# Neighbourhood attention: one key order for both layouts, scores as 64-row products, the next pair's scores before this pair's mix

## The chip, the cores and the metric

The kernel runs on one core of one Trainium2 chip. The metric is device time in microseconds. Three runs of the kernel before gave a median of 2800.92 us (2799.02 to 2803.72). The core has five engines with instruction queues of their own: PE multiplies matrices (weights are loaded by separate instructions, PEld in the profile), DVE and ACT work elementwise from SBUF and PSUM, POOL works elementwise from SBUF, and SP issues transfers. [...]

## The reference

The program is a two-layer encoder over 16 meta tokens and 512 grid tokens, 2048 wide. The first layer (a state-space branch and a convolution branch) is not touched here. The second is a neighbourhood attention with 32 heads of 64: each token of an 8 x 64 grid sees all 8 rows of 16 columns around it, and the 16 meta tokens. Cut to what matters:

```
def neighbourhood_attention(q, k, v, rpb):
    ...
    def row_block(r):
        rs = jnp.clip(r - kh // 2, 0, rows - kh)
        k_rows = lax.dynamic_slice_in_dim(kg, rs, kh, axis=1)
        ...
        s = jnp.einsum("bqhd,bjkhd->bhqjk", q_row, k_rows).astype(jnp.float32) * scale
        ...
        s = s + jnp.transpose(bias, (0, 2, 1, 3))[None]
        s = jnp.where(col_mask[None, None, :, None, :], s, -jnp.inf)
        ...
        s_m = jnp.einsum("bqhd,bkhd->bhqk", q_row, km).astype(jnp.float32) * scale
        p = jax.nn.softmax(jnp.concatenate([s, s_m], axis=-1), axis=-1).astype(v.dtype)
        o = (jnp.einsum("bhqj,bjhd->bqhd", p[..., :kh * GRID_W], ...)
             + jnp.einsum("bhqm,bmhd->bqhd", p[..., kh * GRID_W:], vm))
```

The layer then computes `o * silu(z)`, where z is the fourth part of the input projection, the output projection, the residual, and a final norm.

## The kernel before

Everything is kept transposed: channels on the 128 partitions, tokens along the free dimension, grid tokens ordered column by column (8 rows of a column lie together). Products that need fp32 precision are made of three products in a reduced format: each operand is split into a high part (a rounded copy, made by ACT) and a low part (the rest, made by DVE), and high x high, high x low and low x high are summed in PSUM. This holds for the projections (`fetch`, line 189 on: `wh` by ACT at L196, `wl` by DVE at L199) and for the scores.

**Stage.** Queries, keys and values lie in DRAM (`vqk_d`) when the attention stage begins. It goes over 16 pairs of heads; one pair fills the 128 partitions, head 0 on the lower 64, head 1 on the upper 64. The 512 queries are cut into four windows of 128 queries (16 grid columns); a window needs 24 or 32 grid columns of keys and the 16 meta keys, 208 or 272 keys in all (NK is 272).

**A pair, before.** `Pair` loads keys, queries and values into single buffers (`tk`, `tq`, `vT`) and the bias strips of both heads (`bt`). `khigh` and `qhigh` make the high parts on ACT, head by head (L888, L905). `klow` (L890) makes the low part of the keys and then, on DVE, the copies that the products need: the keys of the two inner windows laid out with the meta keys ahead (`wins`, L853 and L855), and the high part copied to the other 64 partitions (L896). `qlow` (L907) writes the low part of the queries to the other 64 partitions. With that, one product of 128 rows computes high x high and low x high of a head together (L946), and one of 64 rows adds high x low (L947):

```
nc.tensor.matmul(pq[:, :NK], self.qs[a][:, w * P:(w + 1) * P], self.kk[a][:, cb:cb + NK], start=True, stop=False)
nc.tensor.matmul(pq[:, :NK], self.qs[a][hs, w * P:(w + 1) * P], self.kl[hs, cb:cb + NK], start=False, stop=True)
```

`bias` builds the bias and mask of a window on POOL (L931). A DVE instruction adds it to the scores and takes the extreme of each row (L949), ACT takes the exponential and the sum (L950), `norm` scales the rows (L958), `turn` transposes them on PE into PSUM (L969 to L977) and copies them to SBUF (DVE L978 and L981, ACT L979 and L980), `values` transposes the values (L919, L921), and `mix` multiplies both (L994). The result leaves PSUM on ACT (L996).

**Order.** PE, DVE, ACT and POOL follow the order written out in the loop at L1065; SP's order is chosen by the planner. Between the steps of a pair, `next(g)` puts chunks of twelve products of the gate's projection (L1008), so that PE has work of its own while the other engines prepare; each pair has four chunks. After every second pair, `silu` (L1025) applies SiLU to two gate panels on ACT, multiplies the outputs of two pairs on POOL (L1029) and stores them. In the last pair, `reload` and `refill` bring the gated outputs back for the output projection, whose first panel's chunks come from the same generator. The loop's order per pair is: scores of head 0, chunk, scores of head 1, norm, chunk, transposes of head 0, chunk, transposes of head 1, values and key preparation of the next pair, chunk, query preparation, mix.

PSUM has five rotating buffers under the tag `sm` for scores, transposed probabilities and transposed values, and one for the mix.

## Time and profile before

| | |
|---|---|
| median of 3 runs | 2800.92 us (2799.02 to 2803.72) |
| span of the profiled execution | 2800.9 us |
| PE busy | 2706.6 us, 97% |
| DVE busy | 2241.9 us, 80% |
| ACT busy | 1419.8 us, 51% |
| POOL busy | 518.7 us, 19% |
| first and last chunk of the gate's projection (L1008) | 2187.9 and 2613.6 us |
| transfers | 354.23 MB, mean 126 GB/s |

The profiled execution's own time is its span. A busy PE counts from the start of a product to its modelled end, and products overlap, so the busy share does not show how densely products follow each other; the distance between their starts does. PEclk in the views is the clock that PE was granted, 1.00 for full speed. In a timeline row stand the start, the duration, the engine, the line, and what the instruction writes and reads with its shape; "x4" means that rows of one kind were merged, and a bracket gives the idle time before it and what ended it. The chain of waits follows the end of the program back: each piece is what the rest waited for.

### The profile page before, as it was taken

To read this page: it belongs to the slowest core of one execution; us is meant where nothing else is said; L and a number is where in the kernel's file an instruction comes from. 1 tells how busy PE (TensorE), PEld (TensorE's weight loads), DVE (VectorE), ACT (ScalarE), POOL (GpSimd) and SP (SyncE) were. 2 spreads that over 40 slices of the span, in tenths; PEclk is the share of its full clock that TensorE was granted. 3 is DMA by queue.
4 is the path that set the end of the run, shared out by engine and by line. 5 is a ranking of instruction groups with operands and counts; after the bars stand their busy time and mean duration, and the time that the engine had idled before them with its cause. 6 is when DMAs were issued, how large, how long until landed. Compare 5 with 4: busy or idle time off the path is not lost. (4 is left out here: it accounts for less than half of the span.)

```text
span 2800.9 us, 52378 instructions
## 1 busy us (share of the span) xinstructions
PE 2706.6 (97%) x21100; PEld 2548.9 (91%) x21100; DVE 2241.9 (80%) x3182; ACT 1419.8 (51%) x2601; POOL 518.7 (19%) x495
## 2 busy tenths in 40 slices
PE   8999999999999999999999899999999999999897
PEld 8999999999999999999999899999999776766797
DVE  7786786968769699977888898888888876776786
ACT  5356576565765664256435355333333554555443
POOL 2000000000000011002334323212212323222322
PEclk9999999999999999999999999999999998998998
DMA  4222222222222224337547466333333533333644
GB/s 163 89 82 84 88 80 89 86 89 86 78 95 80 95 83 147 107 131 252 161 147 252 157 205 211 131 135 119 133 129 125 143 94 95 99 94 109 204 158 152
DMA packets 133218, 354.23 MB, mean 126 GB/s; under 512 B 15488, under 2 KB 27904, under 8 KB 132976
## 3 DMA queue, kind: packets, MB, share of 16 engines
q1 hardware_dynamic: 126144, 328.65, 36.6%
q0 software_dynamic: 6544, 22.17, 2.2%
q8 instruction: 165, 2.70, 0.4%
q14 instruction: 77, 0.63, 0.1%
q10 hardware_dynamic: 288, 0.07, 0.0%
HBM read 300.40 MB, written 50.43 MB: 125 GB/s over the span
## 5 line engine op out<-in xcount | busy, mean ns | idle before, releaser
L196 ACT ACTIVATE wh<-raw 128x1024 fp32r<-128x1024 f32 (+1 forms) x458 | 484.0, 1058 | 731.3 <-PE pb L216 281.1
L235 PE MATMUL ps<-rh,wh 128*128 128x264 f32 (+2 forms) x3536 | 739.7, 288 | 13.7 <-ACT rh L252 8.5
L235 PE MATMUL ps<-rh,wl 128*128 128x264 f32 (+2 forms) x3536 | 739.8, 288 | 0.5 <-DVE wl L199 0.5
L235 PE MATMUL ps<-rl,wh 128*128 128x264 f32 (+2 forms) x3536 | 735.8, 288 | 1.2 <-DVE rl L253 1.1
L199 DVE TENSOR_TENSOR wl<-raw,wh 128x1024 fp32r<-128x1024 f32 (+1 forms) x458 | 582.0, 1271 | 96.0 <-ACT wh L196 89.1
L235 PEld LDWEIGHTS ps<-rh,wh 128*128 128x128 f32 (+1 forms) x3536 | 555.0, 189 | 20.2 <-ACT rh L252 8.5
L235 PEld LDWEIGHTS ps<-rh,wl 128*128 128x128 f32 (+1 forms) x3536 | 554.4, 189 | 4.2 <-DVE wl L199 1.2
L235 PEld LDWEIGHTS ps<-rl,wh 128*128 128x128 f32 (+1 forms) x3536 | 552.2, 189 | 5.7 <-DVE rl L253 2.0
L216 PE MATMUL pb<-rh,wl 128*128 128x264 f32 (+1 forms) x1280 | 368.2, 288 | 12.0 <-DVE wl L199 11.5
L216 PE MATMUL pb<-rh,wh 128*128 128x264 f32 (+1 forms) x1280 | 367.0, 287 | 4.1 <-ACT wh L196 3.8
L216 PE MATMUL pb<-rl,wh 128*128 128x264 f32 (+1 forms) x1280 | 366.3, 286 | 0.0
L529 DVE SCALAR_TENSOR_TENSOR a<-up,prm,a 128x528 f32<-128x528 f32 x464 | 345.2, 775 | 2.3 <-ACT a L524 0.9
L216 PEld LDWEIGHTS pb<-rh,wl 128*128 128x128 f32 x1280 | 243.3, 190 | 16.3 <-DVE wl L199 16.1
L216 PEld LDWEIGHTS pb<-rh,wh 128*128 128x128 f32 x1280 | 244.4, 191 | 5.7 <-ACT wh L196 5.5
L216 PEld LDWEIGHTS pb<-rl,wh 128*128 128x128 f32 x1280 | 244.1, 191 | 0.0
L216 PE MATMUL pb<-ta,wh 128*128 128x264 f32 (+1 forms) x1280 | 235.9, 284 | 2.5 <-ACT wh L196 2.4
L216 PEld LDWEIGHTS pb<-ta,wh 128*128 128x128 f32 x1280 | 198.4, 189 | 3.8 <-ACT wh L196 3.8
L216 PE MATMUL pb<-ta,wl 128*128 128x264 f32 (+1 forms) x640 | 180.8, 285 | 0.5 <-DVE wl L199 0.2
L196 ACT ACTIVATE wh<-S 128x1024 fp32r<-128x1024 f32 x80 | 84.5, 1057 | 120.0 <-PE pb L216 87.9
L216 PE MATMUL pb<-tb,wh 128*128 128x264 f32 (+1 forms) x640 | 125.6, 293 | 10.3 <-ACT tb L1142 5.8
L931 POOL TENSOR_TENSOR bm<-cst,bt 128x256 f32<-128x256 f32 (+1 forms) x128 | 94.0, 763 | 201.0 <-DVE mx L949 195.4
L1008 PE MATMUL ps<-rh,wh 128*128 128x512 f32 x272 | 121.2, 445 | 1.1 <-ACT rh L249 1.1
(324 smaller groups left out, 4337.0 us busy)
## 6 DMA issues: line engine op xcount, KB each, us to landing
raw<-win SPq DMA_DIRECT2D x192, 512.0 KB, 3.7
raw<-oin SPq DMA_DIRECT2D x128, 512.0 KB, 3.7
raw<-wout SPq DMA_DIRECT2D x64, 512.0 KB, 4.1
raw<-oout SPq DMA_DIRECT2D x32, 512.0 KB, 3.8
srt<-h_d SPq DMA_DIRECT2D x38, 264.0 KB, 4.4
srt<-yz_d SPq DMA_DIRECT2D x32, 264.0 KB, 5.3
srt<-yb_d SPq DMA_DIRECT2D x32, 264.0 KB, 4.0
vqk_d<-cx SPq DMA_DIRECT2D x26, 264.0 KB, 2.0
```

What stands on the lines that cost most here:

```text
L196: nc.scalar.activation(wh, raw, AF.Copy)
L199: nc.vector.tensor_tensor(wl, raw, wh.bitcast(F32), op=ALU.subtract)
L216: nc.tensor.matmul(o, w[:, k, :], u[:, lo:lo + n], start=(k == 0 and j == 0), stop=(k == KH - 1 and j == 2))
L235: nc.tensor.matmul(ps[:M, n, :N], w[:, k, :], u[:, lo + n * N:lo + (n + 1) * N], start=(kk == 0 and j == 0), stop=(kk == KT - 1 and j == 2))
L529: nc.vector.scalar_tensor_tensor(a, u[:, j:j + L], wv(j), a, op0=ALU.mult, op1=ALU.add)
L931: nc.gpsimd.tensor_tensor(bm[:, n0:n0 + n * GR].rearrange("p (c r) -> p c r", r=GR), am[:, w, c0:c0 + n].unsqueeze(2).to_broadcast([P, n, ...
L1008: nc.tensor.matmul(ps, w[:, k, :], u[:, lo:lo + S], start=(kk == 0 and j == 0), stop=(kk == KT - 1 and j == 2))
```

## The change

The keys and values get one order in SBUF, with the meta tokens in it twice: columns 0 to 63 of the grid, the 16 meta tokens, grid columns up to 464, the meta tokens again, and the last 64. Every window is then one contiguous stretch (`WIN`), and three transfers each for `tk` and `vT` write that order, so that the copies on DVE go. The high and low parts are made for both heads at once, each head staying on its own 64 partitions (`high`, `low`). Scores are three products of 64 rows for each window and head, 24 a pair instead of 16, and the heads, and so the partition halves, alternate. They are 208 columns wide for the outer windows and 272 for the inner ones. `tk`, `tq`, `vT` have two buffers, `bt` four, and the bias tiles four for each window; an outer window's bias is now written by two POOL instructions, on both sides of the meta columns.

The loop's order changes too: bias of the next pair, both norms of this pair, transposes of head 0, high parts of the next pair, chunk, low parts, transposes of head 1, values, chunk, scores of the next pair's outer windows, chunk, scores of its inner windows, this pair's mix, SiLU, chunk. The first pair's scores stand ahead of the loop. In the last pair, twelve outputs are reloaded at its start instead of eight and later four, and the refills move with the chunks.

```diff
+WIN = ((0, 208, ((0, 0, 8), (80, 8, 16)), 64), (64, NK, ((16, 0, WC),), 0), (208, NK, ((0, 0, WC),), 256), (336, 208, ((0, 8, 16), (144, 24, 8)), 128))
...
-TQB = 1
...
-        bms = {}
-        for w, n, lo in ((0, 2, 0), (1, 3, 0), (3, 2, 192)):
-            wd_ = NM + (192 if w != 1 else 256)
-            bms[w] = [ak.tile([P, wd_], F32, name=f"bm{w}{i}") for i in range(n)]
+        bms, bmi = [], [0] * NWIN
+        for w, (_, n, _, m) in enumerate(WIN):
+            bms.append([ak.tile([P, n], F32, name=f"bm{w}{i}") for i in range(4)])
             for t in bms[w]:
-                nc.gpsimd.memset(t[:, lo:lo + NM], 0.0)
-        bms[2] = bms[1]
-        bmi = {id(bms[w]): 0 for w in (0, 1, 3)}
+                nc.gpsimd.memset(t[:, m:m + NM], 0.0)
...
-        def wins(dst, src, rows):
-            d = dst[:, 2 * NK:].rearrange("p (w n) -> p w n", w=2)
-            nc.vector.tensor_copy(d[:, :, NM:], bass.AP(tensor=src.tensor, offset=src.offset + 80,
-                                                        ap=[list(src.ap[0]), [P, 2], [1, 256]]))
-            nc.vector.tensor_copy(d[:, :, :NM], src[:, :NM].unsqueeze(1).to_broadcast([rows, 2, NM]))
-        GEO = ((NM, 24, 0, 0, 208), (NM, WC, 0, 0, NK), (NM, WC, 0, 0, NK), (0, 24, 8, 64, NK))
         VSL = ((0, 128), (80, 208), (208, 336), (336, 464), (128, 208), (464, 544))
-        FULL = ((0, 0), (1, 16), (1, 144), (2, 16), (2, 144), (3, 64))
+        FULL = ((0, 0), (1, 16), (1, 144), (2, 0), (2, 128), (3, 0))
+        META = ((1, 0), (2, 256))
...
-                self.vT = ak.tile([P, L + NM], F32, name="vT", tag="vT", bufs=1)
-                self.tq = ak.tile([P, S], F32, name="tq", tag="tq", bufs=TQB)
-                self.tk = ak.tile([P, L + NM], F32, name="tk", tag="tk", bufs=TQB)
-                nc.sync.dma_start(self.tk[:, :L], vqk_d[3 * p + 2])
-                nc.sync.dma_start(self.tq, vqk_d[3 * p + 1, :, NM:])
-                nc.sync.dma_start(self.vT[:, :L], vqk_d[3 * p])
+                self.vT, self.tk = (ak.tile([P, L + NM], F32, name=n, tag=n, bufs=2) for n in ("vT", "tk"))
+                self.tq = ak.tile([P, S], F32, name="tq", tag="tq", bufs=2)
+                for t, i in ((self.tk, 3 * p + 2), (self.tq, 3 * p + 1), (self.vT, 3 * p)):
+                    if t is self.tq:
+                        nc.sync.dma_start(t, vqk_d[i, :, NM:])
+                        continue
+                    src = vqk_d[i]
+
+                    def two(ap, o, step, n):
+                        return bass.AP(tensor=ap.tensor, offset=ap.offset + o, ap=[list(ap.ap[0]), [step, 2], [1, n]])
+
+                    nc.sync.dma_start(t[:, 80:464], src[:, 80:464])
+                    nc.sync.dma_start(two(t, 0, 480, 64), two(src, NM, 448, 64))
+                    nc.sync.dma_start(two(t, 64, 400, NM), two(src, 0, 0, NM))
                 self.bt = []
                 for a in range(2):
-                    t = ak.tile([P, RUN], F32, name="bt", tag="bt", bufs=2)
+                    t = ak.tile([P, RUN], F32, name="bt", tag="bt", bufs=4)
                     src = bass.AP(tensor=rpb.tensor, offset=rpb.offset + (2 * p + a) * 465 + 16,
                                   ap=[[1, KW], [31, GR], [1, RUN]])
                     nc.sync.dma_start(t, src)
                     self.bt.append(t)
-                self.bm, self.sb, self.sm, self.rg, self.pT = {}, {}, {}, {}, {}
-            def khigh(self):
-                t = self.tk
-                nc.vector.tensor_copy(t[:, L:], t[:, :NM])
-                nc.vector.tensor_copy(self.vT[:, L:], self.vT[:, :NM])
...
-            def klow(self, a):
...
-                wins(self.kk[a][x], kf[x], HD)
-                nc.vector.tensor_copy(self.kk[a][y], kf[x])
-                if a:
-                    wins(self.kl, self.kl.bitcast(F32), P)
...
-            def qhigh(self):
...
-            def qlow(self):
-                    nc.vector.tensor_tensor(self.qs[a][y], t[x], self.qs[a][x].bitcast(F32), op=ALU.subtract)
+                self.bm, self.sb, self.sm, self.mx, self.pT = {}, {}, {}, {}, {}
+
+            def high(self):
+                self.kh, self.kl = (ak.tile([P, L + NM], F32R, name=n, tag=n, bufs=2) for n in ("kh", "kl"))
+                self.qh, self.ql = (ak.tile([P, S], F32R, name=n, tag=n, bufs=2) for n in ("qh", "ql"))
+                nc.scalar.activation(self.kh, self.tk, AF.Copy)
+                nc.scalar.activation(self.qh, self.tq, AF.Copy)
+
+            def low(self):
+                for l, t, h in ((self.kl, self.tk, self.kh), (self.ql, self.tq, self.qh)):
+                    nc.vector.tensor_tensor(l, t, h.bitcast(F32), op=ALU.subtract)
...
-            def bias(self, a):
+            def bias(self):
                 for w in (0, 3, 1, 2):
-                    bl = bms[w]
-                    bm = bl[bmi[id(bl)] % len(bl)]
...
-            def scores(self, a):
...
-                for w in (0, 3, 1, 2):
...
-                    cb = (0, 544, 816, 272)[w]
-                    nc.tensor.matmul(pq[:, :NK], self.qs[a][:, w * P:(w + 1) * P], self.kk[a][:, cb:cb + NK], start=True, stop=False)
-                    nc.tensor.matmul(pq[:, :NK], self.qs[a][hs, w * P:(w + 1) * P], self.kl[hs, cb:cb + NK], start=False, stop=True)
...
+                    for a in range(2):
+                        bm = bms[w][bmi[w] % 4]
+                        bmi[w] += 1
+                        for at, c0, n in WIN[w][2]:
+                            bv = bass.AP(tensor=self.bt[a].tensor, offset=self.bt[a].offset + SOFF[w] - c0,
+                                         ap=[list(self.bt[a].ap[0]), [-1, n], [-31, GR]])
+                            nc.gpsimd.tensor_tensor(bm[:, at:at + n * GR].rearrange("p (c r) -> p c r", r=GR),
+                                                    am[:, w, c0:c0 + n].unsqueeze(2).to_broadcast([P, n, GR]), bv, op=ALU.subtract)
+                        self.bm[a, w] = bm
+
+            def scores(self, ws):
+                if not self.sb:
+                    for a in range(2):
+                        self.sb[a] = ap.tile([P, NWIN, NK], F32, name="sb", tag="sb", bufs=SBB)
+                        self.mx[a] = ap.tile([P, NWIN], F32, name="mx", tag="mx", bufs=2)
+                        self.sm[a] = ap.tile([P, NWIN], F32, name="sm", tag="smt", bufs=2)
+                pqs = {}
+                for w in ws:
+                    st, n = WIN[w][:2]
+                    for a in range(2):
+                        pqs[a, w] = psb.tile([P, 512], F32, name="pq", tag="sm", bufs=SMB)
+                    for j, (x, y) in enumerate(((self.qh, self.kh), (self.ql, self.kh), (self.qh, self.kl))):
+                        for a in range(2):
+                            hs = slice(a * HD, (a + 1) * HD)
+                            nc.tensor.matmul(pqs[a, w][:, :n], x[hs, w * P:(w + 1) * P], y[hs, st:st + n], start=(j == 0), stop=(j == 2))
+                for a in range(2):
+                    for w in ws:
+                        n = WIN[w][1]
+                        sv, mx = self.sb[a][:, w, :n], self.mx[a][:, w:w + 1]
+                        nc.vector.tensor_tensor_reduce(sv, pqs[a, w][:, :n], self.bm[a, w], 1.0, BIG * 4, ALU.add, ALU.min, mx)
+                        nc.scalar.activation(sv, sv, AF.Exp, bias=mx, scale=-1.0, accum_out=self.sm[a][:, w:w + 1])
...
-                    nc.vector.tensor_scalar_mul(self.rg[a][w], self.rg[a][w], sm[:, w:w + 1])
+                    sv = self.sb[a][:, w, :WIN[w][1]]
+                    nc.vector.tensor_scalar_mul(sv, sv, sm[:, w:w + 1])
...
-                nc.tensor.transpose(pb[:80, 3 * P:4 * P], sb[:, 3, 192:272], ident)
-                for w in (1, 2):
-                    nc.tensor.transpose(self.po[:NM, (2 * a + w - 1) * P:(2 * a + w) * P], sb[:, w, :NM], ident)
+                nc.tensor.transpose(pb[:80, 3 * P:4 * P], sb[:, 3, 128:208], ident)
+                for w, c in META:
+                    nc.tensor.transpose(self.po[:NM, (2 * a + w - 1) * P:(2 * a + w) * P], sb[:, w, c:c + NM], ident)
...
-                                lt, rt = self.vt[:NM, 0, hs], self.pm[:, a, w - 1]
+                                lt, rt = self.vt[:NM, 5, hs], self.pm[:, a, w - 1]
...
-        tags = ("vT", "tq", "tk", "kl", "kk0", "kk1", "qs0", "qs1")
+        tags = ("vT", "tq", "tk", "kl", "kh", "qh", "ql")
...
-                tg = tags[k % 8]
-                w = {"tq": S, "vT": L + NM, "tk": L + NM}.get(tg, S if tg[0] == "q" else 4 * NK)
-                t = ak.tile([P, w], F32, name="ord", tag=tg, bufs=1 if k % 8 < 3 else 2)[:, :S]
+                tg = tags[k % 7]
+                t = ak.tile([P, S if tg[-1] == "q" or tg[0] == "q" else L + NM], F32, name="ord", tag=tg, bufs=2)[:, :S]
...
             cur = Pair(0)
-            cur.khigh()
-            cur.qhigh()
-            cur.klow(0)
-            cur.klow(1)
-            cur.qlow()
-            cur.bias(0)
+            cur.high()
+            cur.low()
+            cur.bias()
             while len(halves) < AHEAD and (todo or pend):
                 fetch()()
             g = filler()
             next(g)
             cur.values()
+            cur.scores((0, 3))
             next(g)
-            fetch()()
+            cur.scores((1, 2))
             for p in range(KT):
                 nxt = Pair(p + 1) if p + 1 < KT else None
                 o = ap.tile([P, S], F32, name="o", tag="o", bufs=4)
                 os_.append(o)
-                cur.scores(0)
-                cur.bias(1)
-                next(g)
-                cur.scores(1)
+                if nxt:
+                    nxt.bias()
+                else:
+                    reload(0, 12)
                 cur.norm(0)
+                cur.norm(1)
+                cur.turn(0)
                 if nxt:
-                    nxt.bias(0)
-                else:
-                    reload(0, 8)
-                next(g)
-                cur.turn(0)
-                if not nxt:
-                    refill(0, 4)
-                cur.norm(1)
+                    nxt.high()
                 low = fetch()
-                if nxt:
-                    nxt.qhigh()
                 next(g)
                 if nxt:
-                    nxt.khigh()
+                    nxt.low()
+                else:
+                    refill(0, 4)
                 low()
                 cur.turn(1)
-                if not nxt:
-                    refill(4, 8)
-                    reload(8, 12)
-                    silu((KT - 2, KT - 1))
                 if nxt:
                     nxt.values()
+                next(g)
                 if nxt:
-                    nxt.klow(0)
+                    nxt.scores((0, 3))
+                else:
+                    refill(4, 8)
+                low = fetch()
+                next(g)
+                low()
+                if nxt:
+                    nxt.scores((1, 2))
+                    cur.mix(o)
+                else:
+                    silu((KT - 2, KT - 1))
+                    refill(8, 14)
+                    cur.mix(o, zts[p])
                 if p % 2 == 0 and p:
                     silu((p - 2, p - 1))
-                low = fetch()
-                if nxt:
-                    nxt.klow(1)
                 next(g)
-                if nxt:
-                    nxt.qlow()
-                low()
-                if nxt:
-                    cur.mix(o)
-                else:
-                    refill(8, 14)
-                    cur.mix(o, zts[p])
                 cur = nxt
+            refill(14, 16)
             next(g)
-            refill(14, 16)
+            fetch()()
             next(g)
```

37 lines of the change are left out of this document (removed).

## Prediction

> **What bounds the kernel now.** I read the page first, then the chain of waits inside the attention stage, the waits of that stage, and the timeline of one pair of head pairs on each engine. The page says that PE is busy nearly throughout:
>
> ```profile
> span 2800.9 us, 52378 instructions
> PE 2706.6 (97%) x21100; PEld 2548.9 (91%) x21100; DVE 2241.9 (80%) x3182; ACT 1419.8 (51%) x2601; POOL 518.7 (19%) x495
> ```
>
> The span equals the median of the runs (2800.92), so there is nothing around it to add, and the sum below is made against 2800.9. The change touches only the attention stage. The chain of waits, in order of time, shows its rhythm. Each `po L994 x40` is one pair's mix, so the distance between two of them is the period of a pair:
>
> ```profile
> 2190.86 2.68 issue
> ...
> 2216.63 2.93 PE po L994 x40
> ...
> 2238.88 2.93 PE po L994 x40
> ...
> 2416.57 1.06 DVE qs L911
> 2422.00 4.19 PE ps L1008 x12
> 2428.55 2.99 PE ps L1008 x12
> ...
> 2542.09 2.93 PE po L994 x40
> ```
>
> Pairs 0 to 1 take 2238.88 - 2216.63 = **22.25 us**, and there the chain stays on PE. Pairs 1 to 13 take (2542.09 - 2238.88) / 12 = **25.27 us** each. The difference of 3.02 us has two parts. In every second pair the chain leaves PE and runs through the DVE copies of the keys and the low half of the queries. The waits of the stage give that its size:
>
> ```profile
> PE pq L946 <- DVE qs L911: 15.0, 7, 2.2
> ```
>
> Seven waits, 2.2 us the longest. The rest is the clock. Microsecond by microsecond (PE busy, granted clock, DMA share, GB/s):
>
> ```profile
> 2416.00:2417.00 1.00, 0.00 (x0) 1.00 0.67 259
> ...
> 2418.00:2419.00 1.00, 1.00 (x3) 0.50 0.00 0
> ...
> 2446.00:2447.00 1.00, 1.00 (x3) 0.50 0.93 360
> ```
>
> After the wait at 2416 the clock is half, which stretches a chunk of twelve products (4.19 against 2.99 in the chain). It also halves around 2446, where PE did not wait at all: there mix and the slowly issued scores lie back to back. So two pairs lose 2 x 3.02 = 6.0, of which 2.2 is the wait and nearly 4 the clock, and thin PE work can drop the clock alone.
>
> Why DVE is late every second pair: the products with the SiLU gate run on POOL just then, and the same copy takes 2.5 times as long.
>
> ```profile
> 2410.89 0.72 DVE L896 CAST kk<-kk 64x1088 fp32r<-64x1088 f32 x1
> 2412.83 1.80 DVE L896 CAST kk<-kk 64x1088 fp32r<-64x1088 f32 x1
> ```
> ```profile
> 2412.76 2.99 POOL L1029 TENSOR_TENSOR o<-o,z 128x512 f32<-128x512 f32 x2 [10.71 <-ACT z L1027]
> ```
>
> **The change, part by part.**
>
> *Scores.* Now 16 products a pair, one of 128 rows and one of 64 in turn. The PE timeline of an undisturbed pair, with rows from elsewhere for comparison:
>
> ```profile
> 2393.25 0.39 PE L946 MATMUL pq<-kk,qs 128*128 128x272 f32 x1
> 2393.57 0.39 PE L947 MATMUL pq<-kl,qs 64*128 64x272 f32 x1
> ...
> 2395.81 0.50 PE L1008 MATMUL ps<-rh,wh 128*128 128x512 f32 x1
> ...
> 2398.70 0.29 PE L946 MATMUL pq<-kk,qs 128*128 128x272 f32 x1
> ...
> 2401.16 0.50 PE L1008 MATMUL ps<-rh,wh 128*128 128x512 f32 x1
> ```
> ```profile
> 2000.17 0.28 PE L216 MATMUL pb<-rh,wl 128*128 128x264 f32 x1
> 2000.29 0.28 PE L216 MATMUL pb<-rh,wh 128*128 128x264 f32 x1
> ```
> ```profile
> 98.57 0.87 PE L394 MATMUL pt<-cst,dt 64*88 64x64 f32 x12
> ```
> ```profile
> 2381.81 0.60 PE L969 MATMUL pa<-cst,sb 128*128 128x128 f32 x4
> 2382.25 0.38 PE L973 MATMUL pb<-cst,sb 128*128 128x128 f32 x2
> ...
> 2390.32 1.10 PE L994 MATMUL po<-pT,vt 128*64 128x128 f32 x16
> 2391.35 0.43 PE L994 MATMUL po<-pm,vt 16*64 16x128 f32 x4
> 2391.71 0.66 PE L994 MATMUL po<-pT,vt 128*64 128x128 f32 x8
> ```
>
> A block of eight takes 2395.81 - 2393.25 = 2.56 and 2401.16 - 2398.70 = 2.46, together **5.02 us a pair**, 0.32 a product. The same width without a change of row count takes 0.12 (2000.17 to 2000.29). So 0.2 of each 0.32 is paid for going from 128 rows to 64 and back. In the mix the same change, 128 rows to 16, costs about 0.14: four products take 0.36 (2391.35 to 2391.71) where sixteen last 0.44 more than eight, 0.055 each. Twelve 64-row products in a row, of 64 columns, take 0.87 to the end of the last, 0.07 each at most, so 64 rows as such are not slow.
>
> The new scores are 24 products of 64 rows, 208 or 272 columns, alternating between the upper and lower row half; the row count changes only around the two blocks. No row shows alternating row halves, so I bound it. One product at a time at 0.12 for 264 columns is 0.095 and 0.124, mean 0.11: 24 x 0.11 + 4 x 0.14 = 3.2. If the two halves run side by side, half of that: 24 x 0.055 + 0.56 = 1.9. The far end is the 0.32 of today: 24 x 0.32 = 7.7. Near the low ends lies the mix, which alternates column halves without a penalty: 0.055 a product of 128 columns against (2382.25 - 2381.81) / 4 = 0.11 for a transpose of 128 columns on the full array. I take 0.085 between the two near bounds: 24 x 0.085 + 0.56 = 2.6, so **2.4 us a pair saved, 38 us over 16 pairs** (29 to 50; far end +43).
>
> [...]
>
> *The stall.* Removed from DVE per pair: the two 1088-wide copies, the window copies, the two small copies of meta columns, and one each of the two key and query subtractions, which now cover 128 partitions at once.
>
> ```profile
> L896 DVE CAST kk<-kk 64x1088 fp32r<-64x1088 f32 x31 | 29.5, 951 | 1.1
> L911 DVE TENSOR_TENSOR qs<-tq,qs 64x512 fp32r<-64x512 f32 x32 | 27.5, 858 | 1.0
> ...
> L853 DVE CAST kl<-kl 128x512 fp32r<-128x512 f32 x16 | 14.7, 917 | 0.2
> ```
>
> These rows alone give 2 x 0.95 + 0.92 + 0.86 = 3.7 us; the window copies of the keys, one key subtraction and the narrow copies come on top. More important is the place: the remaining subtractions come after the first chunk of the iteration's four, and the scores that need them come two chunks and the second head's transposes later. So the wait goes; what is late next? I followed the longest chain in the new order, in a pair after SiLU, where the exponential's table must be reloaded:
>
> ```profile
> L199 DVE TENSOR_TENSOR wl<-raw,wh 128x1024 fp32r<-128x1024 f32 x35 | 43.3, 1240 | 4.6 <-ACT wh L196 4.1
> L949 DVE CUSTOM_DVE_ANT_0 sb<-pq,bm 128x272 f32<-128x272 f32 x64 | 28.2, 441 | 16.6 <-PE pq L947 16.4
> L958 DVE TENSOR_SCALAR sb<-sb,sm 128x272 f32<-128x272 f32 x64 | 26.1, 448 | 0.0
> ```
> ```profile
> L196 ACT ACTIVATE wh<-raw 128x1024 fp32r<-128x1024 f32 x34 | 35.8, 1052 | 18.8 <-PE ps L1008 17.0 <-issue 1.8
> L950 ACT ACTIVATE sb<-sb,mx 128x272 f32<-128x272 f32 x64 | 33.2, 519 | 3.0 <-DVE mx L949 0.2
> L950 ACT ACT_TABLE_LOAD x8 | 10.3, 1283 | 32.3 <-DVE mx L949 29.3 <-DMA vqk_d<-cx 3.0
> ```
>
> From the first score block: table 1.28, four exponentials 2.1, the weight's high part 1.05 on ACT; behind it, in DVE's order, the weight's low part 1.24, four score reductions 1.8, the first head's normalisation 1.8. That is 9.3 us, from about 0.6 before the block's end. PE has until the transposes a chunk 2.9, a block 1.3, mix 2.9 and a chunk 2.9, 10.0 us. About 1.3 us to spare, so nothing shows; without that cover each microsecond would show at the transposes. **All 14 disturbed intervals recover their 3.02 us: 42 us.**
>
> *Loads and bias.* Keys and values come as three transfers each, nine issues a pair for five; SP's own waits in the stage are for buffers, which are now doubled. POOL gets twelve bias operations for eight, some of them smaller, off the path: it waits most of the time now, and the wait for the score reductions goes with four buffers. In the first pair POOL must bias both heads before the second block.
>
> ```profile
> SPq L876 <- POOL bm L931: 114.6, 30, 7.8
> ```
> ```profile
> POOL bm L931 <- DVE mx L949: 195.4, 31, 14.1
> ```
>
> I cost both at nothing, with the loads issued most of a pair ahead as cover; if they came late, the price is that of the moved stall below.
>
> *Ends.* Pair 0's second block is followed at once by its transposes: the same reductions, exponentials and normalisation stand bare, about 3 us, and one half-clock stretch of 1.5. The 2.68 of the chain's "issue" piece, where PSUM was held by the backlog on DVE, may shrink by half. Net +3. The last pair's work only changes its order: 0, between -5 and +5.
>
> *Clock left over.* The second block and the mix, 4.2 us of part-array work, now lie together: +4, a few drops.
>
> **Sum:** 2800.9 - 42 - 38 + 3 + 4 = **2728 us**. With the near bounds of the scores and the ends, 2712 to 2746.
>
> **The rivals.**
>
> 1. *Row halves fully side by side*: 2800.9 - 42 - 50 + 7 = **2716**. For it: the mix's column halves. Against it: a weight load of 128 columns stands ahead of each product, and no row shows how fast those can follow each other below 0.11.
>
> 2. *The clock falls in every pair* after second block and mix. For it: the drop at 2446 without a wait. Against it: that drop had 0.32-spaced scores, which stream 272 columns only a third of the time, and the new block is dense. Price: 4.19 - 2.99 = 1.2 for the chunk and some 0.3 beside it, 1.5 a pair: 2728 + 24 - 4 = **2748**; with two such stretches **2772**. [...]
>
> 3. *The stall moves* to the first score block: its PSUM bank waits for a DVE copy queued behind the weight's low part, behind the query subtraction, behind a late key load. For it: SP issues in order, and stores of gated outputs that wait for POOL may stand ahead of the loads. Against it: the query and key subtractions are a chunk and more ahead of the block. Price as today, 42 us: **2770**.
>
> [...]
>
> **How the numbers follow.** Forecast 0.45, rival 1 0.20, rival 2 0.13, rival 3 0.09, rival 4 0.08 with the clock's fall and 0.05 without. A measurement of this kernel tells about 0.2% (5.6 us) from no change. Faster 0.45 + 0.20 + 0.13 + 0.09 = 0.87, same 0.05, slower 0.08. The range 2704 to 2780 holds the forecast and the first three rivals but for their tails, and leaves out rival 4.
>
> **What would show it.** Right: product starts in a score block 0.055 to 0.11 apart; pair periods near 19.9 and no alternation; no PE wait on DVE of a microsecond or more after pair 0; granted clock near 1.0 through the stage against 0.50 in stretches now; DVE busy over 4 us a pair less. Wrong: spacing near 0.3; clock dips after each mix; PE waits before the first score block or the first transposes. If the period falls but the time does not, the tail has taken it: look at the reloads of the outputs and the first chunk of the output projection.

## The result, and the profile after

The changed kernel takes 2708.26 us (median; 2702.53 to 2709.69) against 2800.93: a ratio of **0.9666, interval 0.9652 to 0.968**, 93 us less. The forecast was 2728, within 2704 to 2780. Its profiled execution has a span of 2705.7, so 95.2 us less than the 2800.9 of before:

```profile
span 2705.7 us, 52618 instructions
...
PE 2630.5 (97%) x21228; PEld 2508.7 (93%) x21228; DVE 2147.2 (79%) x2990; ACT 1389.0 (51%) x2567; POOL 528.5 (20%) x568
```

PE is as busy as before by its share; DVE is 95 us less busy (2241.9 before), 5.9 a pair. The chain of waits of the stage, with the mixes (now L974) and, late in the stage, one pair's pieces:

```profile
2242.67 2.93 PE po L974 x40
2261.80 2.93 PE po L974 x40
2280.95 2.93 PE po L974 x40
2300.46 2.93 PE po L974 x40
...
2474.41 2.93 PE po L974 x40
...
2489.17 0.85 PE pq L925 x12
...
2493.01 0.95 PE pq L925 x11
...
```

The period of a pair is 19.15 or 19.55 us (2261.80 - 2242.67 = 19.13; 2300.46 - 2280.95 = 19.51), where it was 22.25 and 25.27 on the mean. The two score blocks last 0.85 and 0.95, **1.80 a pair against 5.02**. The PE timeline of one block, the outer windows of 208 columns, shows why:

```profile
2392.14 0.36 PE L925 MATMUL pq<-kh,qh 64*128 64x208 f32 x2
2392.34 0.28 PE L925 MATMUL pq<-kh,ql 64*128 64x208 f32 x2
2392.46 0.27 PE L925 MATMUL pq<-kl,qh 64*128 64x208 f32 x2
```

Each row is two products, one of each row half, and a row comes every 0.11 us: 0.056 a product, the near end of the forecast's bounds. In the block of the inner windows (272 columns) a row comes every 0.125, 0.0625 a product. The waits of PE from the stage to the end:

```profile
PE pq L925 <- DVE mx L930: 9.3, 1, 9.3
PE pb L216 <- ACT wh L196: 4.3, 4, 2.9
...
PE pa L949 <- POOL bm L907: 2.7, 1, 2.7
...
```

The seven waits for the queries' low part are gone, and so are two groups of waits in the output projection that the kernel before had:

```profile
PE pb L216 <- ACT tb L1142: 5.8, 2, 5.3
...
PE ps L235 <- DVE fo L1182: 3.3, 1, 3.3
```

New, and large, are two single waits at the start of the stage, 9.3 and 2.7 us. The granted clock, with those behind it, is 0.66 from 2200 to 2220 and 1.00 in each stretch from there to 2500, of which the first is shown:

```profile
2200.00:2220.00 20.00, 15.24 (x75) 11.59 (x76) 12.33 (x36) 9.51 (x27) 6.20 (x14) 0.66 0.47 113
2220.00:2320.00 100.00, 100.00 (x722) 78.62 (x722) 63.13 (x182) 58.54 (x152) 35.99 (x61) 1.00 0.41 116
```

(In each row: PE, PEld, DVE, ACT and POOL busy time, then granted clock, DMA share, GB/s.)

**Where the 95.2 us lie.** The mix of pair 1 starts at 2238.88 before and 2242.67 after. At that point before still has pair 2's scores to do (5.02) and after one chunk more (2.98), so at equal work the clock stands at 2243.90 and 2245.65: 1.75 lost, although three pairs' scores have already saved 3 x 3.10 (the difference of the periods 22.25 and 19.15). The start therefore costs 11.0. From the mix of pair 1 to that of pair 13: 303.21 before, 2474.41 - 2242.67 = 231.74 after, 71.5 gained; 12 x 3.10 = 37.2 of it is scores, 34.3 waits and clock. Behind pair 13, at equal work, 253.8 before and 228.3 after, 25.5 gained: 3.1 scores, about 2 x 2.86 = 5.7 waits and clock (34.3 / 12 a pair), and some 16.7 in the last pair and the output projection (the 5.7 and the 16.7 are estimates, from the 2.86 a pair). In sum: scores 49.6, waits and clock 40.0, end 16.7, start -11.0.

The start holds one thing that isn't the change's doing. The stage's first chunk begins at 2187.91 before and at 2184.29 after, 3.6 us earlier, although the work ahead of the stage is the same. Over the profiled executions of this document it begins anywhere from 2182.4 to 2188.3; in the run with the gate's products on DVE, whose program is that of before up to there, at 2182.5. Counted from the first chunk, the start costs 14.6, and 3.6 of the 95.2 lie ahead of the stage. Where times at the start of the stage are compared below, this has to be kept in mind.

### The profile page after: what moved, and what is told of

It is laid out like the page before. It is cut to its first block, busy times and chain, and to the rows that moved or that the text cites. A ratio compares the mean times of both kernels' runs of the same rounds, so it can differ in the third digit from the quotient of the medians.

```text
span 2705.7 us, 52618 instructions
## 1 busy us (share of the span) xinstructions
PE 2630.5 (97%) x21228; PEld 2508.7 (93%) x21228; DVE 2147.2 (79%) x2990; ACT 1389.0 (51%) x2567; POOL 528.5 (20%) x568
## 4 chain that ended last, share of the span: by engine, by line
PE 73%; DVE 8%; issue 7%; DMA 5%; ACT 4%; POOL 3%; SPq 0%; DVEq 0%; POOLq 0%; ACTq 0%
PE ps L235 38%; PE pb L216 19%; PE ps L988 7%; DVE wl L199 2%; PE po L974 2%; PE py L506 2%; PE pq L925 1%; PE st L446 1%; ACT wh L196 1%; POOL srt L782 1%; DVE a L529 1%; DVE S L163 1%; DVE raw L167 1%; DMA raw<-oout 1%; DMA raw<-oin 1%
## 5 line engine op out<-in xcount | busy, mean ns | idle before, releaser
L199 DVE TENSOR_TENSOR wl<-raw,wh 128x1024 fp32r<-128x1024 f32 (+1 forms) x458 | 593.3, 1295 | 123.9 <-ACT wh L196 117.7
L216 PEld LDWEIGHTS pb<-ta,wl 128*128 128x128 f32 x640 | 120.5, 189 | 1.5 <-DVE wl L199 1.5
L988 PE MATMUL ps<-rh,wh 128*128 128x512 f32 x272 | 114.3, 420 | 0.0
```

The source lines that it names most:

```text
L199: nc.vector.tensor_tensor(wl, raw, wh.bitcast(F32), op=ALU.subtract)
L216: nc.tensor.matmul(o, w[:, k, :], u[:, lo:lo + n], start=(k == 0 and j == 0), stop=(k == KH - 1 and j == 2))
L988: nc.tensor.matmul(ps, w[:, k, :], u[:, lo:lo + S], start=(kk == 0 and j == 0), stop=(kk == KT - 1 and j == 2))
```

## The experiments

All ratios are to the kernel before, run beside it. The first four take the change apart.

### New products without the new order

The changed kernel with the loop's old order: each pair's scores at the start of its own iteration, preparation at the old places.

```diff
             for p in range(KT):
...
+                cur.scores((0, 3))
+                next(g)
+                cur.scores((1, 2))
+                cur.norm(0)
...
-                    nxt.scores((0, 3))
...
-                    nxt.scores((1, 2))
                     cur.mix(o)
```

> The changed kernel with the old order of the loop: products, loads, bias and buffers are the new ones, but each pair's scores stand at the start of its own iteration, and its high and low parts at the old places. Theory (the order hides the preparation, not only the missing copies): DVE still makes the low parts after the second head's transposes, one chunk ahead of the scores, beside POOL's SiLU products in every second pair; a wait of about 1 us there and half clock behind it in seven pairs, so 3.5 to 5.5 us in two pairs, 2735 to 2750. Rival (taking the copies away suffices): the copies took about 6.5 us of DVE a pair, three times the longest wait of 2.2, so no wait is left; pair period 19.2 to 20 without the new order, and the bare start of the new order (9.3 us of wait before the first mix) goes; 2697 to 2715.

Measured: 2734.82 us, ratio 0.9769 (0.9749 to 0.9789). The time is within 0.2 us of the theory's low end, the place is not the theory's. After the first pair PE waits at the transposes, in four pairs, not at the scores:

```profile
PE pa L949 <- DVE sb L938: 13.8, 4, 4.5
```
```profile
2341.80 6.58 DVE L938 TENSOR_SCALAR sb<-sb,sm 128x208 f32<-128x208 f32 x4
```
```profile
2332.37 2.50 POOL L1009 TENSOR_TENSOR o<-o,z 128x512 f32<-128x512 f32 x2 [23.41 <-DMA vT<-vqk_d]
2334.84 12.63 POOL L907 TENSOR_TENSOR bm<-cst,bt 128x64 f32<-128x64 f32 x24
```

The four scalings of a head take 1.11 us when POOL is idle. Here they take 6.58, because POOL, which has stood behind SiLU for 23 us (the bracket names a load, but the product starts as ACT's SiLU, from 2331.66, delivers), writes two pairs' bias in one stretch of 12.6 us just then. The chain of waits shows that it is the first of the four that waits:

```profile
2341.80 5.81 DVE sb L938
```

It ends at 2347.6, and POOL's stretch at 2334.84 + 12.63 = 2347.47; the other three take 0.8 together. So a new theory: what the old order loses in the stage, it loses to POOL's bias beside the normalisation. The last experiment tests it.

### The new order without the new products

The kernel before, with its copies, single buffers and products, in the new order; the first head's scores of the next pair ahead of the last chunk before the mix, the second head's behind it.

```diff
+                    nxt.khigh()
+                    nxt.qhigh()
...
+                    nxt.klow(0)
+                    nxt.klow(1)
+                    nxt.qlow()
...
+                    nxt.scores(0)
+                    nxt.bias(1)
...
+                    nxt.scores(1)
+                    cur.mix(o)
```

> The kernel before with the new order alone: copies, single buffers and the 128-row and 64-row products of before stay; the next pair's scores, head by head, stand ahead of this pair's mix. Theory (the gain of the stall is from the copies first; the order moves the scores nearer to the preparation's end than the copies allow): the copies of about 6.5 us a pair end later than the scores are due, a PE wait of 1 to 4 us in every second pair or in each, half clock behind it, 2790 to 2850. Rival (the order alone hides the preparation, copies and all): the period is that of an undisturbed pair before, 22.25 us, so 42 us less and 11 for the start, 2760 to 2775. A clock that falls after each mix, where the slow second block of scores (2.5 us) lies against the mix, without a wait of PE before it, would show that thin work alone drops the clock; about 1.5 us a pair, 24 us.

Measured: 2784.47 us, ratio 0.9941 (0.9919 to 0.9964): 6 us below the theory's range, with its mechanism. The wait stays, as often and a little longer, and the copies are in the chain ahead of it:

```profile
PE pq L946 <- DVE qs L911: 17.6, 7, 2.6
```
```profile
2380.64 1.02 DVE kl L894
...
2383.27 1.11 DVE kk L896
```

The order alone doesn't hide the copies. This run also bears on the second rival (the clock falls in every pair): the slow second block of scores, 0.32 a product, lies right against the mix here, and the clock stays full over both:

```profile
2421.00:2424.00 3.00, 3.00 (x36) 2.05 (x38) 2.65 (x13) 1.83 (x8) 0.00 (x0) 1.00 0.51 175
```

Together:

| | old products and copies | new products, no copies |
|---|---|---|
| old order | 1 | 0.9769 |
| new order | 0.9941 | 0.9666 |

The new products, here together with the new loads and the doubled buffers, are worth 65 us of 2801 by themselves, the order 16 by itself and 29 on top of them. By the profiled spans the 29 are 24.8 (2730.5 - 2705.7): 19.1 between the mixes of pairs 1 and 13 (250.88 against 231.74), 14.2 behind them, and 8.5 the other way at the start. Loads and buffers were not tried apart from the products.

### The gate's products on DVE, in the kernel before

```diff
-                    (nc.gpsimd if q < KT - 2 else nc.vector).tensor_tensor(os_[q], os_[q], zts[q], op=ALU.mult)
+                    nc.vector.tensor_tensor(os_[q], os_[q], zts[q], op=ALU.mult)
```

> The kernel before, with the products of the outputs with the SiLU gate all on DVE instead of POOL. Theory (the stall came from DVE copies stretched while POOL works, 0.72 to 1.80 us): the copy beside SiLU takes 0.7 to 0.9 again, the wait of 2.2 falls below 0.5, the clock holds, the alternating of the periods ends; two products of about 0.6 us on DVE come on top in two pairs; 2760 to 2775. Rival (DVE is late because it has too much to do in every second pair, whatever POOL does): 1.2 us more on DVE makes the wait 2 to 3.5 us and the time 2800 to 2812.

Measured: 2797.8 us, ratio 0.9992 (0.9977 to 1.0006), no change; neither theory has it. The stretching goes, but the products stand in DVE's own queue, where they wait 1.1 us for ACT and take 1.3:

```profile
2410.88 1.29 DVE L1029 TENSOR_TENSOR o<-o,z 128x512 f32<-128x512 f32 x2 [1.11 <-ACT z L1027]
...
2413.40 0.72 DVE L896 CAST kk<-kk 64x1088 fp32r<-64x1088 f32 x1
```
```profile
PE pq L946 <- DVE qs L911: 10.7, 6, 1.8
```

The copy is back at 0.72 from 1.80, and the longest wait is 1.8 for 2.2. What POOL took from DVE and what the move puts on it are nearly the same: before, DVE had no room in that pair.

### The three products of a head in turn

```diff
-                    for j, (x, y) in enumerate(((self.qh, self.kh), (self.ql, self.kh), (self.qh, self.kl))):
-                        for a in range(2):
+                    for a in range(2):
+                        for j, (x, y) in enumerate(((self.qh, self.kh), (self.ql, self.kh), (self.qh, self.kl))):
```

> The changed kernel with the loops over heads and products exchanged: the three products of one head's window follow each other on the same row half, then the three of the other. Theory (two row halves run side by side, and need neighbours on different halves): products follow each other at 0.095 (208 columns) and 0.124 (272) within a head, with one overlap per window and one per change of head, so a pair's two score blocks grow from 1.8 to 2.4 to 2.9 us, +0.6 to +1.1 us a pair, 2718 to 2726. Rival (64-row products are fast by themselves, in whatever order): spacing stays near 0.06 and the time within 3 us of 2708.

Measured: 2707.17 us, ratio 0.9665 (0.9651 to 0.9679). The rival's number. But the PE timeline doesn't show its reason:

```profile
2391.92 0.37 PE L925 MATMUL pq<-kh,qh 64*128 64x208 f32 x2
2392.12 0.28 PE L925 MATMUL pq<-kh,ql 64*128 64x208 f32 x2
2392.23 0.28 PE L925 MATMUL pq<-kl,qh 64*128 64x208 f32 x2
```

The rows are still pairs of the same kind, although the program has kh x qh, kh x ql and kl x qh of one head ahead of the first product of the other. So the trace left two readings open: halves that run together in whatever order they come, or products that are fast alone. The next run decides.

### All products on one row half

```diff
-                            hs = slice(a * HD, (a + 1) * HD)
+                            hs = slice(0, HD)
```

> The changed kernel with every score product on the lower row half: the products for head 1 take head 0's queries and keys, so head 1's scores are left out and head 0's computed twice; count, shapes, waits and order stay. Theory (upper and lower row half work at the same time, whatever the order they are issued in): twelve products of 208 and twelve of 272 columns follow each other at about 0.10 and 0.125, the two blocks grow from 1.8 to about 3.2, +1.4 us a pair, 2725 to 2735. Rival (a 64-row product is done in 0.06 by itself): blocks as before, 2703 to 2712.

Measured: 2726.37 us, ratio 0.9727 (0.971 to 0.9743), as the theory has it. A row of two products now comes every 0.25 us, and a pair's blocks are the following:

```profile
2391.18 0.42 PE L925 MATMUL pq<-kh,ql 64*128 64x272 f32 x2
2391.43 0.41 PE L925 MATMUL pq<-kl,qh 64*128 64x272 f32 x2
```
```profile
2386.40 1.52 PE pq L925 x12
2390.89 1.69 PE pq L925 x12
```

One product of 272 columns takes 0.125 on one half, and in the changed kernel two, one on each half, take the same: the row halves run fully side by side. 3.21 - 1.80 = 1.41 a pair, 16 x 1.41 = 23, of which 18 show.

### Two bias tiles for each window instead of four

```diff
-            bms.append([ak.tile([P, n], F32, name=f"bm{w}{i}") for i in range(4)])
+            bms.append([ak.tile([P, n], F32, name=f"bm{w}{i}") for i in range(2)])
...
-                        bm = bms[w][bmi[w] % 4]
+                        bm = bms[w][bmi[w] % 2]
```

> The changed kernel with two bias tiles for each window instead of four, so one pair's worth. POOL can then write the next pair's bias only when this pair's reductions have read theirs, that is beside the normalisation, as in the kernel before (there the first head's four scalings took 2.50 us beside POOL, 1.11 without). Theory (POOL's bias work stretches DVE's scalings, and four tiles matter because they move it away from them): the first four scalings take 2.0 to 2.6 instead of 1.11, +1.4 on the chain to the first transposes, which has nothing to spare in every second pair and about 1.3 in the others: 8 x 1.4 to 15 x 1.4 us more, 2718 to 2732. Rival (POOL's time doesn't matter to DVE): scalings stay at 1.1, 2705 to 2712.

Measured: 2706.55 us, ratio 0.9661 (0.9643 to 0.9678), no change. The stretching comes as foreseen, but in the other pair:

```profile
2382.94 1.11 DVE L938 TENSOR_SCALAR sb<-sb,sm 128x208 f32<-128x208 f32 x4
...
2403.23 2.24 DVE L938 TENSOR_SCALAR sb<-sb,sm 128x208 f32<-128x208 f32 x4
```

In the pair whose chain has nothing to spare POOL stands behind SiLU while DVE scales, so 1.11; in the other it writes bias, 2.24, and that pair has the room. So the time is the rival's, but its reason (POOL doesn't matter to DVE) isn't shown: the scalings do stretch. The four tiles aren't what the gain hangs on.

### The start of the stage

The first reduction of the stage came at 2201.18, 13 us after its scores. I took it that it waited for the last store of queries, keys and values. First, that store earlier:

```diff
-            nc.gpsimd.tensor_tensor(t, t, row, op=ALU.mult)
+            (nc.gpsimd if m < len(vqk) - 2 else nc.vector).tensor_tensor(t, t, row, op=ALU.mult)
```

> The changed kernel with the scaling of the last two rows of the queries, keys and values on DVE instead of POOL, so that their store doesn't stand behind ten bias instructions. Theory (the stage's first reduction waits for that store, whose source lies where the score tiles are put): the store leaves about 6 us earlier, the first reduction comes at about 2193 to 2195 instead of 2201, and the PE wait of 9.3 us there falls below 3; 2698 to 2703. Rival (the bias tiles or the first loads hold the reduction as well): the wait changes its name and the time stays within 3 us of 2708.

Measured: 2701.24 us, ratio 0.9641 (0.9626 to 0.9655). The issue of that store, its landing time and the first reduction, in the changed kernel and then in this one:

```profile
2195.05 0.51 SPq L824 DMA_DIRECT2D vqk_d<-cx  x1
```
```profile
vqk_d<-cx SPq DMA_DIRECT2D x1, 264.0 KB, 5.9
```
```profile
2201.18 0.37 DVE L930 CUSTOM_DVE_ANT_0 sb<-pq,bm 128x208 f32<-128x208 f32 x1 [13.02 <-DMA vT<-vqk_d]
```
```profile
2191.74 0.38 SPq L824 DMA_DIRECT2D vqk_d<-cx  x1
```
```profile
vqk_d<-cx SPq DMA_DIRECT2D x1, 264.0 KB, 5.8
```
```profile
2197.86 0.38 DVE L930 CUSTOM_DVE_ANT_0 sb<-pq,bm 128x208 f32<-128x208 f32 x1 [7.64 <-POOL bm L907]
```

2195.05 + 5.9 = 2200.95, the reduction at 2201.18; 2191.74 + 5.8 = 2197.54, the reduction at 2197.86. The store went out 3.3 us earlier, not 6 as expected, since SP had loads of bias in front of it, and the reduction followed it, whatever the bracket names. PE's wait fell to 5.5, not below 3; the time is within the theory's range. (The first chunks of the two executions lie 0.5 us apart, so they can be compared directly.)

Then one chunk more in the start, one less at the end:

```diff
             cur.scores((1, 2))
+            next(g)
             for p in range(KT):
...
             fetch()()
-            next(g)
```

> The same as the run before (last two rows scaled on DVE), and one more chunk of the gate's projection between the first pair's second score block and its transposes, taken from the end of the stage, where one chunk less is left. Theory (the first pair's transposes stand bare behind reductions, exponentials and norm): the waits there, 2.7 and 0.3 us and the half clock behind them, go; 3 to 6 us less than without the chunk, 2693 to 2699. Rival (the chunk is missed at the end of the stage, where the reloads of the outputs are waited for): no difference to the run before, or up to 3 us more.

Measured: 2705.66 us, ratio 0.9658 (0.9644 to 0.9672): 4 us slower than without it, somewhat beyond the rival's 0 to 3. The waits at the first transposes went, but the output projection waited 7.7 us for its weights' low parts, 2.3 without the chunk moved: the chunk was missed at the end.

Then the wait itself, by moving the score tiles from memory that has to do with the store:

```diff
+        sp_ = c2.enter_context(tc.tile_pool(name="sq", bufs=1))
         ap = c2.enter_context(tc.tile_pool(name="ap", bufs=1))
...
-                        self.sb[a] = ap.tile([P, NWIN, NK], F32, name="sb", tag="sb", bufs=SBB)
+                        self.sb[a] = sp_.tile([P, NWIN, NK], F32, name="sb", tag="sb", bufs=SBB)
```

(`mx` and `sm` alike; the lines behind the first stand one further on in this run and the next two.)

> The changed kernel with the score tiles and their row results in an SBUF pool of their own, which no longer lies over the memory from which the last rows of queries, keys and values are stored; nothing else is touched. Theory (the stage's first reduction waits for that store to land, because the score tiles' pool as a whole reuses its source's memory: store issue plus landing was 2195.05 + 5.9 = 2200.95 and the reduction came at 2201.18): the reduction comes when bias and scores are there, 2188 to 2193, the PE wait of 9.3 us falls below 2, and a wait of 2 to 4 us stays at the first transposes, which stand bare; 2697 to 2702. Rival (POOL's bias, 2194.7 at the latest for the first pair, sets it): the reduction at about 2195 and 2702 to 2706.

Measured: 2696.92 us, ratio 0.962 (0.9604 to 0.9635), 11 us below the changed kernel, about the whole cost of its start. From the first chunk (2187.8 here) to the mix of pair 1 at equal work, 48.5 us pass, against 61.4 in the changed kernel and 56.0 before. The reduction no longer waits, and comes before the store's source has even been scaled:

```profile
2192.11 0.36 DVE L931 CUSTOM_DVE_ANT_0 sb<-pq,bm 128x208 f32<-128x208 f32 x1
```
```profile
2196.44 1.32 POOL L823 TENSOR_TENSOR cx<-cx,rsa 128x528 f32<-128x528 f32 x1
```
```profile
PE pa L950 <- DVE sb L939: 2.2, 1, 2.2
```

Of the waits of 9.3 and 2.7, the 2.2 at the transposes are left, about what the forecast had for the whole start. So the first reduction waited for the memory that it wrote to, not for its operands. Whether the score tiles themselves lay where the store reads, or only their pool did, this run doesn't tell, since it moves both.

Both remedies together, and then the second fetch's weights made after the second block's exponentials and reductions:

```diff
-                low = fetch()
+                if not nxt:
+                    low = fetch()
                 next(g)
-                low()
+                if not nxt:
+                    low()
                 if nxt:
                     nxt.scores((1, 2))
+                    low = fetch()
+                    low()
```

> The pool of its own and the scaling of the last two rows on DVE together. Theory: with the store off the path, what the scaling on DVE still gives is two fewer POOL instructions (2.3 and 1.3 us) ahead of the first pair's bias; the reduction at 2188 to 2191, 0 to 3 us less than with the pool alone, 2695 to 2700. Rival (both are the same wait): the same as the pool alone within 2 us.

> The run before this one, and the weights' high and low parts of each pair's second fetch made after the second score block's exponentials and reductions instead of ahead of them. Theory (in every second pair the chain from table load over exponentials, weights and reductions to the transposes is about 0.4 us too long: periods of 19.55 beside 19.15): 1.05 us on ACT and 1.24 on DVE leave that chain, all periods become 19.15, 7 x 0.4 = 2.8 us less, 2692 to 2698. Rival (the weights are then missed by the next chunk or by the output projection): waits of PE on the weights' low part, 0 to 10 us more.

Measured: 2695.06 us, 0.9616 (0.9597 to 0.9635), for both remedies, so the rival's "same within 2 us" as well as the theory's low end; the reduction comes at 2187.24, five microseconds earlier by the clock, but in this execution the whole stage begins 5.4 earlier (first chunk at 2182.4 against 2187.8): from the first chunk it is 4.8 against 4.3, no gain. PE waits 6.0 for the first pair's scalings, against 2.2. With the weights later 2695.08 us, 0.9612 (0.9596 to 0.9627). The periods did what the theory said, all alike:

```profile
2306.46 2.93 PE po L975 x40
2325.59 2.93 PE po L975 x40
2344.74 2.93 PE po L975 x40
```

19.14 in every pair, so the 0.4 us left in every second pair was that chain. The profiled span is 2691.8 against 2694.4 for the run before; the medians don't tell the two apart, so the 2.8 us of the theory are seen in the periods and not in the time. These two are the fastest versions, 13 us below the changed kernel, but only 2 below the pool alone, within the scatter of the runs.

### The old order, with POOL out of SiLU

The first experiment again (new products, old order), with the gate's products on DVE, the edit shown above.

> The old order with the new products (the run of 2734.8), and the SiLU gate's products on DVE instead of POOL. Theory (that run lost its time where POOL, held up behind SiLU, then wrote two pairs' bias in one stretch of 12.6 us over the normalisation: four scalings took 6.58 us there): POOL no longer waits for SiLU, writes the bias right after each pair's reductions, and the scalings beside it take 2.2 to 2.6 at most; the 13.8 us of waits at the transposes fall below 4, the half clock behind them goes; 2710 to 2722. Rival (the old order is slow because the preparation stands too near the scores): waits as before or longer for the 1.3 us more on DVE, 2733 to 2745.

Measured: 2714.81 us, ratio 0.968 (0.9663 to 0.9697), as the theory has it: 20 us less than with the products on POOL, from the edit that gave the kernel before nothing. POOL no longer waits for SiLU and writes one pair's bias at a time; no wait at the transposes is longer than 0.3, 4.3 in all (the theory had them below 4):

```profile
2337.30 2.95 POOL L907 TENSOR_TENSOR bm<-cst,bt 128x64 f32<-128x64 f32 x8 [12.60 <-DVE mx L930]
2341.26 3.12 POOL L907 TENSOR_TENSOR bm<-cst,bt 128x256 f32<-128x256 f32 x4 [1.01 <-DVE mx L930]
```
```profile
PE pb L216 <- ACT tb L1110: 5.6, 2, 3.6
...
PE pa L949 <- DVE sb L938: 4.3, 13, 0.3
...
PE ps L235 <- DVE fo L1150: 2.6, 1, 2.6
```

From the mix of pair 1 to that of pair 13 it takes 236.72 us, where the old order took 250.88 with POOL behind SiLU and the new order 231.74: 14.2 of the 19.1 are back. The other 5.0 are 0.4 a pair, with a wait of 0.3 in nearly each.

## Why the prediction was right, and where it was not

**The stall and its clock (forecast 42, measured 40.0).** Right in size, and in place: no PE wait on DVE of a microsecond in any pair after pair 0, clock 1.00 from 2220 on. The chain that I gave 1.3 us to spare is the one that shows: 0.4 too long in every second pair, which the run with the weights later took away. The reason given, that the removal of DVE's copies and the place of the rest go together, holds by the table of the four: neither part reaches the sum alone. What I didn't see is why the place matters. I argued with the distance from the low parts to the scores; the runs show that without copies that distance is enough in the old order too (no wait at the scores after the first pair), and that most of what the new order changes in the stage, 14.2 of 19.1, is when POOL's long stretch of bias meets DVE's scalings. In the changed kernel the stretch lies between two normalisations, and nothing in the loop sees to that:

```profile
2386.00 13.68 POOL L907 TENSOR_TENSOR bm<-cst,bt 128x64 f32<-128x64 f32 x24
```

**The scores (forecast 38, measured 49.6).** The term was mis-sized. I took 0.085 us a product between 0.11 and 0.055; it is 0.056 to 0.0625, both halves side by side, the first rival's mechanism, with its 1.9 us a pair (measured 1.80). The mix's column halves, which I named as the low row, were the right row, and the run on one row half agrees (0.125 us for one product or for one on each half). The argument against, a weight load of 128 columns ahead of each product, didn't hold: in the changed kernel two loads of 0.19 us start with every row, every 0.11 us.

**The ends (forecast +3 and 0, measured +11.0 and -16.7).** Here the steps failed, in opposite directions. At the start I reckoned with bare work of 3 us and put the stall of before, 2.68 of "issue", down to a backlog on DVE, of which half might go. The traces bear that reading out, and all of it went, not half: before, the transposes of the values started 0.1 us after DVE's last sum of the projection ahead of the stage, which stood behind the key copies; after, that sum ends at 2186.23 and PE doesn't stop there; the new order with the old copies stops again, for 3.1.

```profile
2193.54 0.85 PE L919 MATMUL ptv<-cst,vT 128*128 128x128 f32 x6 [2.68 <-issue]
```
```profile
2193.02 0.42 DVE L717 TENSOR_TENSOR cx<-cx,pb 128x264 f32<-128x264 f32 x1
```

What the step left out is the wait for the store's landing. Before, the first reduction came at the same time (2201.11), but there it cost DVE 0.88 us and PE nothing. Scores that stand ahead of the loop moved PE right up against it. The queue that I passed over was POOL's, where the store's scaling stands behind ten bias instructions, and SP's behind it. At the end I expected nothing. The old order costs there: both runs with it and the new products keep the waits for `tb` and `fo` (7.3 and 2.8 us in the first, 5.6 and 2.6 in the second), which the new order doesn't have, and their time from pair 13's mix to the end, at equal work, is 14 and 13 us longer (242.5 and 241.2 against 228.3). The new order with the old products doesn't have these waits either. Which of the moved reloads and refills does it wasn't tried.

**Clock left over (forecast +4).** None. The dense second block next to the mix didn't lower the clock in any pair from 2220 to 2500, nor did the slow scores of before ahead of the mix in the run with the order alone (1.00 both times), so the second rival has nothing left here. The fall at 2446 in the kernel before (to 0.50, without a wait beside it) stays unexplained; that thin work drops the clock by itself was my estimate from that one fall, and no run shows it.

**The sum.** The errors are 11.6 on the scores, 16.7 at the end and 4 on the clock in the one direction, 8 at the start and 2 on the waits in the other: 22.3, the distance from 2728 to the span of 2705.7. That 2728 kept within its range is in part luck: the errors of one sign came to 32.3 us, those of the other to 10, and without the 10 the time would have fallen below 2704. (With the start counted from the first chunk, the 10 are 13.6, and 3.6 ahead of the stage join the other side.) The narrower 2712 to 2746 of the forecast doesn't follow from its terms either: 2728 - 12 - 5 = 2711 and 2728 + 9 + 5 = 2742. The third rival (the stall moves to the first score block) and the fourth (a change of row half costs what a change of row count does, 0.32 a product) are refuted by the waits and by the spacing (0.056 to 0.0625). That SP issues in order, which I held for the third, shows in the kernel before: beside SiLU the load of `tk` went out at 2414.48, behind a store at 2414.06 and 2.1 us after the buffer's last reader ended (2412.36); a pair earlier, without SiLU, at once (2390.14 after 2390.11).

## What to carry to other kernels

Price a product from rows that use the array in the same way, here the mix's column halves, before taking a middle value, and test it by putting all of it on one half. Where DVE is late, look first at what POOL does in that microsecond: the same scalings cost 1.1 or 6.6 us, and most of what the old order lost in the stage hung on that. When a stage is made denser, its first instruction deserves a look of its own: a wait for a store's landing cost 11 us here, and a pool of its own for the tiles used first gave them back.

## What the runs showed of the hardware

**Two row halves pair up by themselves.** In the run with the heads in turn, products that stand three apart in the program start together by the records, 2391.92 for the first of both heads. So whole products seem to be taken ahead of others. No run shows whether the engine does that and how far ahead it looks, or whether a later step of the build exchanges the instructions.

**DVE slows beside POOL, by kind of instruction.** Scalings (1.11 for four, 6.58 beside POOL), copies (0.72 and 1.80) and the subtractions (0.67 and 0.97 for the queries') stretch; the reductions, which read PSUM, keep their 0.44 throughout (0.43 to 0.44 at 2339.95 to 2341.05 in the old order, beside POOL). One scaling stood for 5.81 us there, until POOL's stretch of bias ended, and the other three took 0.8 together, so DVE seems to have waited and not merely worked more slowly. POOL's 24 bias instructions took 0.53 us in the mean (12.63 in all), so about eleven of them went by in that time, an estimate from these numbers. In the last experiment, beside bias instructions of 0.8 us (3.12 for four), no scaling stood that long: three in the chain of waits took 1.97 together. What DVE waits for, and why it waits so much longer in the one than in the other, no run shows.

**A change of row count cost about 0.2 us, a change of half nothing.** 0.32 a product where 128 and 64 rows alternate, 0.12 for 128 rows throughout (264 columns), both in the kernel before; 0.125 for 64 rows on one half, 0.0625 on both in turn in the changed kernel (272 columns). The 0.2 is an estimate, 0.32 less 0.12.
